# Gate decays of a linear-attention stage as products with constant 0/1 matrices, without scans

## The chip, the core and the metric

The kernel runs on one core of one Trainium2 chip. The metric is the device time of one execution in microseconds (us): the kernel before takes 1326.52 us, the median of three runs from 1323.62 to 1327.46.

Engine names in this text: PE is the matrix engine and PEld its weight loads, DVE the vector engine, ACT the scalar engine with the exponentials, POOL the third elementwise engine, SP the queue that issues DMAs.

## The reference

One layer of a diffusion backbone over 1024 latent tokens and 256 context tokens of width 1024. A mixer has two head groups side by side, gated linear attention (GLA, 4 heads, keys of 64, values of 128) and a state-space group (SSD); behind them come an output projection and a SwiGLU part. Shifts, scales and gates of both halves come from a modulation vector (`w_mod`). The change is in the GLA group, which runs forward and backward over the tokens:

```python
g_f = log_sigmoid(lr_f @ gla_wg_f + gla_bg_f) / 16.0        # g_b likewise; lr has 16 columns a direction

def step(s, inp):                                           # one chunk of _gla_scan
    qc, kc, vc, gc = inp
    cum = jnp.cumsum(gc, axis=1)
    inter = einsum("blhk,bhkv->blhv", qc * exp(cum), s)
    diff = cum[:, :, None] - cum[:, None, :]
    decay = exp(where(mask, diff, -inf))                    # lower triangle
    att = einsum("bihk,bjhk,bijhk->bhij", qc, kc, decay)
    intra = einsum("bhij,bjhv->bihv", att, vc)
    tot = cum[:, -1]
    s_new = s * exp(tot)[..., None] + einsum("blhk,blhv->bhkv", kc * exp(tot[:, None] - cum), vc)
    return s_new, inter + intra
```

So five things need exponentials of sums of gate steps `g`: queries against the state (`cum`), keys into the state (`tot - cum`), the whole chunk (`tot`), and for pairs of tokens inside a chunk the difference of two `cum`, split between query and key.

## The kernel before, in words

The program is one list of steps for all engines. Tile pools and a scheduler put each engine's instructions in an order; each engine then works its own list from the top. The GLA part works in two passes over pairs of heads, `gla_pair(p)` for p = 0 and 1, with 128 channels of a pair on the partitions and the 1280 tokens (`TT`) in ten chunks of 128.

`gates(p)` (L1080) makes, per direction `d`, the running sums of the gate steps, channel-major: three matmuls of `W96` with `LRT` (L1093), two DVE passes, Exp and Ln on ACT over all 1280 columns, one more DVE pass, and a scan along the tokens that a mask of ones and zeros (`rmask`) starts anew in each chunk. It leaves `cum[0]` and `cum[1]`.

Everything else takes differences of `cum`. `khat(d)` makes the keys into the state: DVE subtracts, ACT takes the exponential, POOL multiplies with `kT`, and ten transposes on PE turn the result token-major in `states(d)`, where 20 matmuls and DVE steps (L1165) run the state through the chunks.

Inside a chunk, pairs of tokens are split by levels, `LEVELS = (64, 32, 16, 8, 4, 2, 1, 0)`: at level 64 one half of a chunk meets the other half, at 32 quarters meet, and at the last a token meets itself. `operands(li)` makes one level's scaled queries `eq` and keys `ek` of 1024 columns: two subtractions on DVE (for `eq`) and two on POOL (for `ek`), an exponential of each on ACT, the product of `eq` with the queries on DVE and that of `ek` with the keys on POOL:

```python
V.tensor_tensor(eq, eq, qp, MUL)                                         # L1200
(V if p == 0 and li == 0 else G).tensor_tensor(ek, ek, kp, MUL)          # L1201
```

`products(li)` (L1204) multiplies `eq` with `ek` on PE in 64 matmuls of 64 columns, f32, and `place` (L1218) puts the wanted part into `Ad` with predicated copies on DVE. After the last level `At` holds a chunk's whole table. Then `qe` (queries against the state), and `outputs(hh, i)` (L1268): four groups of twelve f32 matmuls of `At`, `qe`, `St` and `v`, an RMS norm and the gate `r`.

Other work is put between these steps. `F` is a list of projections (units v, k, q, r, z; `proj` with three f16 matmuls of a split product, L198 to L200, called k1, q1 and so on for pair 1), from which `F.fill(us)` takes some steps and `F.need(name)` the rest of one unit. Fillers write to two PSUM banks of their own (`pf`); all else turns through six banks with `psum()`. In pair 1 the output projection `wo` (`out_mm`) and side work (`side(n)`) take the fillers' place. Side work loads and splits `w_out` and makes the modulation vectors: `mod_steps(piece)` (L1001) loads eight row blocks of `w_mod` of 512 KB into a `wst` buffer (L1005) and adds each to `macc` on DVE (L1008, L1010); `mod_row(2)` (L1013) and `mod_col(4)` (L1030) finish them with matmuls against ones, the latter at L1034. Its eight blocks are piece 4. Behind the GLA part `out_tile(t)` finishes 128 tokens of the mixer: it loads `x` (L1353) and stores `x2d` (L1375).

Ahead of the GLA part stands the SSD part, whose pool gives the buffers for masks. Weights that are split into two f16 are made by DVE at L193.

## Time and profile before

| | us | share of the span |
|---|---|---|
| median of three runs | 1326.52 | |
| profiled execution, its own time | 1326.59 | |
| span of its records | 1324.9 | |
| PE busy | 1179.8 | 89% |
| PE weight loads busy | 656.6 | 50% |
| DVE busy | 944.8 | 71% |
| ACT busy | 596.0 | 45% |
| POOL busy | 332.9 | 25% |
| DMA | 139.81 MB, mean 106 GB/s | |

PE is the busy engine over the whole program. A busy share is a mean over stretches of different kinds, so what follows below is cut at the steps of the GLA part: gates of pair 0 from 346.7 us, first product of a level at 380.8, levels of pair 0 to 421.3, its outputs to 472.3, levels of pair 1 to 529.6, its outputs to 578.5, and then the first tiles of `out_tile` to 606.6. The granted clock of PE is given as a share of 2.4 GHz; 0.50 is the other of its two levels, 1.2 GHz, and a stretch between the two holds some of each.

### The profile page before, as it was taken

To read this page: it belongs to the slowest core of one execution; us is meant where nothing else is said; L and a number is where in the kernel's file an instruction comes from. 1 tells how busy PE (TensorE), PEld (TensorE's weight loads), DVE (VectorE), ACT (ScalarE), POOL (GpSimd) and SP (SyncE) were. 2 spreads that over 40 slices of the span, in tenths; PEclk is the share of its full clock that TensorE was granted. 3 is DMA by queue.
4 is the path that set the end of the run, shared out by engine and by line. 5 is a ranking of instruction groups with operands and counts; after the bars stand their busy time and mean duration, and the time that the engine had idled before them with its cause. 6 is when DMAs were issued, how large, how long until landed. Compare 5 with 4: busy or idle time off the path is not lost. (4 is left out here: it accounts for less than half of the span.)

```text
span 1324.9 us, 19466 instructions
## 1 busy us (share of the span) xinstructions
PE 1179.8 (89%) x7640; PEld 656.6 (50%) x7640; DVE 944.8 (71%) x1487; ACT 596.0 (45%) x1104; POOL 332.9 (25%) x245
## 2 busy tenths in 40 slices
PE   5996899999948977977895799999999999999997
PEld 3563565767726666544442344444444444444444
DVE  8688887577699877666679975677775656855347
ACT  5346535445454555342654343444443334443432
POOL 1234051231086273110227311122121111300011
PEclk9997799999968898697997999999999999999999
DMA  9600310101200002447622542355542225320416
GB/s 316 201 18 16 80 45 21 49 1 61 71 33 2 1 1 84 155 157 265 202 76 94 176 143 80 112 175 172 178 143 72 72 80 198 135 100 13 148 67 207
DMA packets 90201, 139.81 MB, mean 106 GB/s; under 512 B 7560, under 2 KB 61053, under 8 KB 90109
## 3 DMA queue, kind: packets, MB, share of 16 engines
q1 hardware_dynamic: 90109, 138.56, 31.9%
q8 instruction: 60, 0.98, 0.3%
q14 instruction: 32, 0.26, 0.1%
HBM read 117.05 MB, written 20.97 MB: 104 GB/s over the span
## 5 line engine op out<-in xcount | busy, mean ns | idle before, releaser
L198 PE MATMUL ps<-T,wS 128*128 128x512 f16 x264 | 102.1, 387 | 14.3 <-DVE u L1566 7.9
L199 PE MATMUL ps<-T,wS 128*128 128x512 f16 x264 | 101.7, 385 | 4.0 <-DVE T L1395 4.0
L200 PE MATMUL ps<-T,wS 128*128 128x512 f16 x264 | 101.6, 385 | 0.0
L1676 DVE TENSOR_TENSOR ah<-hid,ah 128x512 f16<-128x512 f32 x66 | 50.6, 769 | 54.4 <-ACT ah L1675 54.4
L1455 DVE SCALAR_TENSOR_TENSOR wS<-S,wS 128x512 f16<-128x512 f32 x88 | 66.5, 768 | 29.3 <-ACT wS L1454 29.2
L1454 ACT ACTIVATE wS<-S 128x512 f16<-128x512 f32 x88 | 54.3, 628 | 56.1 <-PE ps L200 29.2
L1675 ACT CAST ah<-hid 128x512 f16<-128x512 f32 x66 | 40.4, 617 | 85.3 <-PE ps L200 46.5
L1455 DVE SCALAR_TENSOR_TENSOR wA<-wst,wA 128x512 f16<-128x512 f32 x66 | 54.9, 835 | 29.3 <-ACT wA L1454 29.2
L1454 ACT ACTIVATE wA<-wst 128x512 f16<-128x512 f32 x66 | 41.4, 628 | 59.0 <-PE ps L200 36.3
L1471 POOL TENSOR_TENSOR S<-wst,S 128x512 f32<-128x512 f32 x22 | 32.6, 1483 | 140.2 <-DVE S L1470 88.1
L199 PEld LDWEIGHTS <-wS 128*128 128x128 f16 x352 | 34.9, 99 | 58.0 <-issue 19.1
L198 PEld LDWEIGHTS <-wS 128*128 128x128 f16 x352 | 35.0, 99 | 51.6 <-DVE u L1566 8.4
L1469 POOL TENSOR_TENSOR S<-wst 128x512 f32<-128x512 f32 x22 | 31.0, 1409 | 115.0 <-DVE wS L1455 95.4
L200 PEld LDWEIGHTS <-wS 128*128 128x128 f16 x352 | 35.0, 99 | 47.5 <-issue 7.4
L483 DVE SCALAR_TENSOR_TENSOR acc<-xin,cwcol,acc 128x945 f32<-128x945 f32 (+2 forms) x40 | 50.2, 1273 | 0.4
L1214 PE MATMUL ps<-eq,ek 64*64 64x64 f32 x896 | 22.0, 245 | 29.9 <-DVE ek L1201 14.5
L199 PEld LDWEIGHTS <-hl 128*128 128x128 f16 x448 | 42.8, 98 | 9.9 <-issue 5.5
L198 PEld LDWEIGHTS <-hl 128*128 128x128 f16 x448 | 42.8, 98 | 8.8 <-issue 3.1
L200 PEld LDWEIGHTS <-hl 128*128 128x128 f16 x448 | 42.8, 98 | 5.0 <-issue 0.4
L199 PE MATMUL ps<-wo,oT 128*128 128x512 f16 x112 | 44.4, 397 | 0.0
L198 PE MATMUL ps<-wo,oT 128*128 128x512 f16 x112 | 44.4, 397 | 0.0
L1762 POOL TENSOR_TENSOR ot<-C,macc 128x512 f32<-128x512 f32 x8 | 10.7, 1340 | 133.5 <-PE ps L200 117.9
(538 smaller groups left out, 3667.4 us busy)
## 6 DMA issues: line engine op xcount, KB each, us to landing
wmst<-in_w_mod_dram SPq DMA_DIRECT2D x32, 512.0 KB, 4.2
wst<-in_w_gate_dram SPq DMA_DIRECT2D x26, 512.0 KB, 3.6
wst<-in_w_up_dram SPq DMA_DIRECT2D x26, 512.0 KB, 3.6
wdb<-in_w_down_dram SPq DMA_DIRECT2D x22, 512.0 KB, 5.1
x<-in_x_dram SPq DMA_DIRECT2D x16, 512.0 KB, 6.6
wm<-in_w_mod_dram SPq DMA_DIRECT2D x8, 1024.0 KB, 10.5
t32d<-wdt SPq DMA_DIRECT2D x11, 512.0 KB, 3.4
t14d<-wdt SPq DMA_DIRECT2D x11, 512.0 KB, 4.8
```

Of the source, the lines that this page charges most:

```text
L198: PE.matmul(ps, lh, rh, start=start, stop=False, skip_group_check=on)
L199: PE.matmul(ps, lh, rl, start=False, stop=False, skip_group_check=on)
L200: PE.matmul(ps, ll, rh, start=False, stop=stop, skip_group_check=on)
L483: V.scalar_tensor_tensor(acr[:, r0:r1, q0:q1], xr[:, r0 + dr:r1 + dr, q0 + dc:q1 + dc], cw, acr[:, r0:r1, q0:q1], MUL, ADD)
L1214: PE.matmul(out_[hh][64 * b:64 * b + 64, ci, :], ek[hs, j0:j0 + 64], eq[hs, i0:i0 + 64], start=True, stop=True)
L1454: S.activation(w[:, 0], src, AF.Copy, scale=SW)
L1455: V.scalar_tensor_tensor(w[:, 1], src, SW, w[:, 0], MUL, SUB)
L1469: G.tensor_tensor(s3, b["A11"], b["A21"], SUB)
L1471: G.tensor_tensor(s4, b["A12"], s2, SUB)
L1675: S.copy(dst[:, 0], src)
L1676: V.tensor_tensor(dst[:, 1], src, dst[:, 0], SUB)
L1762: eng.tensor_tensor(ot[:, c0:c0 + n], c, m5r[0][:, m:m + n], MUL)
```

## The change

The gate steps stay token-major and are never summed. For two chunks at a time `gates(p)` multiplies `LRT` (now the stationary side) with `W96` for both directions, adds the bias (loaded as `bt`, broadcast to all partitions), takes the log-sigmoid as min(x, 0) - ln(1 + exp(-|x|)) and scales it by `SG` = 16; `gh` holds it as two f16 parts, the rounded value and the rest.

Every exponent is then a matmul of `gh` with a constant matrix of zeros and ones in f16, one matmul for each part, summed in PSUM (`decay_of`). The running sum of a chunk is `gh` times a triangle (`inc`), what is left to its end is `gh` times the strict triangle (`exc`), the whole chunk is `gh` times a column of ones (`ones16`), and the sums that level `li` needs are `gh` times one of the masks `lvm[:, li]`, which `level_masks()` makes once, in the SSD part, with 28 products on POOL and seven comparisons on DVE. ACT reads the sums from PSUM and takes the exponential with the scale `EG` = 1/256.

So the scans, the subtractions on DVE and POOL and `rmask` go. `khat` works token-major now: the keys `kT` are transposed (ten transposes a pair, not twenty), and DVE multiplies them with the exponentials in PSUM. The products of `ek` are all on DVE. A level of `eq` and `ek` takes four PSUM banks of 512 columns; at level 1 the keys need no factor and `ek` is `kp` itself. In the loop over the levels the sums of level li + 2 are made behind the products of level li, and its factors are applied behind `place`; `khat`, `totals` and `states` stand at other levels than before.

The diff, with short parts left out:

```diff
@@ -36 +36 @@
 SHID = 4.0
 INV = 1.0 / (SW * SH)
 SL = 2048.0
+SG = 16.0
+EG = 1.0 / (16 * SG)
...
@@ -84 +86 @@
...
+    ones16 = cons.tile([P, 1], F16, name="ones16")
+    G.tensor_copy(ones16, ones[:, 0:1])
 
...
@@ -122 +126 @@
...
-    rmask = mc.tile([P, TT], F16, name="rmask")
-    V.memset(rmask, 1.0)
-    V.memset(rmask.rearrange("p (n l) -> p n l", l=P)[:, :, 0:1], 0.0)
+    lvm = mc.tile([P, 7, 2, 2, 64], F16, name="lvm")
+    t16 = mc.tile([P, 4, P], F16, name="t16")
+    inc, exc = (t16[:, 0], t16[:, 1]), (t16[:, 2], t16[:, 3])
+    def level_masks():
...
+        for i, nm in enumerate(("le", "ge", "gt", "lt")):
+            G.tensor_copy(t16[:, i], tri[nm])
+        for li in range(7):
+            lv = 64 >> li
+            bl = ssd.tile([P, P], F16, tag="xw", bufs=3, name="bl")
+            V.tensor_scalar(bl, xi, float(lv), None, ALU.is_lt)
+            b4 = bl.rearrange("p (n a l) -> p n a l", a=2, l=lv)
+            for i, (d, x, a) in enumerate(((0, 0, 1), (1, 0, 0), (0, 1, 0), (1, 1, 1))):
+                G.tensor_tensor(lvm[:, li, d, x].rearrange("p (n l) -> p n l", l=lv),
+                                t16[:, i].rearrange("p (n a l) -> p n a l", a=2, l=lv)[:, :, a], b4[:, :, a], MUL)
...
@@ -725 +748 @@
...
+    level_masks()
...
@@ -1064 +1088 @@
...
-    cums = {}
+    bt = gla.tile([P, 2, 2, P], F32, name="bt")
+    for d, bg in enumerate((gla_bg_f, gla_bg_b)):
+        nc.sync.dma_start(bt[:, :, d], bg.to_broadcast((P, 256)).rearrange("p (q c) -> p q c", q=2))
+    gs = {}
 
     def gates(p):
 
-        cum = cums[p] = []
...
+        gh = gs[p] = gla.tile([P, 2, NCH, 2, P], F16, tag="gh", bufs=1, name=f"gh{p}")
+        for t0 in (2, 4, 6, 8, 0):
+            ps = psum().rearrange("p (t d c) -> p t d c", t=2, d=2)
+            for j in range(2):
+                PE.matmul(ps[:, j], LRT[:, (t0 + j) * P:(t0 + j + 1) * P], W96[:, :, p * P:(p + 1) * P],
+                          start=True, stop=True)
+            x_ = gla.tile([P, 2, 2, P], F32, tag="gx", bufs=2, name="gx")
+            l_ = gla.tile([P, 2, 2, P], F32, tag="gl", bufs=2, name="gl")
+            V.scalar_tensor_tensor(x_.rearrange("p t d c -> p t (d c)"), ps.rearrange("p t d c -> p t (d c)"), INV,
+                                   bt[:, p].rearrange("p d c -> p (d c)")[:, None, :].to_broadcast((P, 2, 256)), MUL, ADD)
+            S.activation(l_, x_, AF.Abs)
+            S.activation(l_, l_, AF.Exp, scale=-1.0)
+            S.activation(l_, l_, AF.Ln, bias=1.0)
+            V.scalar_tensor_tensor(x_, x_, 0.0, l_, ALU.min, SUB)
+            V.tensor_scalar(x_, x_, -4000.0, SG, ALU.max, MUL)
+            S.copy(gh[:, 0, t0:t0 + 2], x_)
+            V.tensor_tensor(gh[:, 1, t0:t0 + 2], x_, gh[:, 0, t0:t0 + 2], SUB)
+            if t0 in (4, 8):
+                F.fill(FILLS[9])
 
     def gla_pair(p, after_levels):
         v = gla.tile([P, NCH, 256], F32, tag="v", bufs=1, name=f"v{p}")
@@ -1115 +1137 @@
         evac_v[0] = False
         if p == 0:
             gates(0)
-        cum = cums[p]
+        gh = gs[p]
         F.need(f"k{p}")
         F.need(f"q{p}")
-        kts, ets, St = [], [], []
...
+        St = []
+        khts = [gla.tile([P, NCH, P], F32, tag="kh", bufs=2, name=f"kht{d}") for d in range(2)]
+        ets = sm.tile([P, 2, NCH], F32, tag="et", name="et")
+        def decay_of(out_, t, d, mask):
+            for s in range(2):
+                PE.matmul(out_, gh[:, s, t, d], mask, start=(s == 0), stop=(s == 1))
+        def khat(n):
+            t0, t1 = ((2, 6), (6, 10), (0, 2))[n]
+            w = (t1 - t0) * P
+            pk = psum()
+            for t in range(t0, t1):
+                PE.transpose(pk[:, (t - t0) * P:(t - t0 + 1) * P], kT[p][:, t * P:(t + 1) * P], ident)
+            for d in range(2):
+                pa = psum()
+                for t in range(t0, t1):
+                    for s in range(2):
+                        PE.matmul(pa[:, (t - t0) * P:(t - t0 + 1) * P], exc[d], gh[:, s, t, d],
+                                  start=(s == 0), stop=(s == 1))
+                kh = khts[d][:, t0:t1].rearrange("p t c -> p (t c)")
+                S.activation(kh, pa[:, :w], AF.Exp, scale=EG)
+                V.tensor_tensor(kh, kh, pk[:, :w], MUL)
+        def totals():
+            pt_ = psum()[:, :2 * NCH].rearrange("p (d n) -> p d n", d=2)
+            for d in range(2):
+                for t in range(NCH):
+                    decay_of(pt_[:, d, t:t + 1], t, d, ones16)
+            S.activation(ets, pt_, AF.Exp, scale=EG)
 
         def states(d):
-            kh, et = kts[d], ets[d]
...
+            kht, et = khts[d], ets[:, d]
             F.fill(FILLS[10])
             F.need(f"v{p}")
             st = gla.tile([P, NL, P], F32, tag=f"St{d}", bufs=1, name=f"St{d}")
@@ -1172 +1207 @@
         Ad = [gla.tile([P, NL, 64], F32, tag="Ad", bufs=2, name=f"Ad{hh}") for hh in range(2)]
         ops = {}
 
+        def decays_of_level(li):
+            lv = LEVELS[li]
+            if li % 2 and lv:
+                eq = ar.tile([P, T], F32, tag="oG", bufs=4, name="eq")
+                ek = ar.tile([P, T], F32, tag="oG", bufs=4, name="ek") if lv > 1 else kp
+            else:
+                eq = gla.tile([P, T], F32, tag="eq", bufs=2, name="eq")
+                ek = gla.tile([P, T], F32, tag="eq", bufs=2, name="ek") if lv > 1 else kp
+            ops[li] = eq, ek
+            if lv == 0:
+                S.activation(eq, qp, AF.Copy, scale=2.0)
+                return
+            for b in range(2):
+                ps = [psum() for _ in range(1 + (lv > 1))]
+                for c in range(4):
+                    t = NC_CTX + 4 * b + c
+                    for d in range(2):
+                        for x_, px in enumerate(ps):
+                            decay_of(px[:, c * P:(c + 1) * P].rearrange("p (n a l) -> p n a l", a=2, l=lv)[:, :, x_ ^ 1 ^ d],
+                                     t, d, lvm[:, li, d, x_].rearrange("p (n l) -> p n l", l=lv))
+                for px, e in zip(ps, (eq, ek)):
+                    S.activation(e[:, b * 512:b * 512 + 512], px, AF.Exp, scale=EG)
         def operands(li):
             lv = LEVELS[li]
-            if li % 2:
...
+            eq, ek = ops[li]
+            if lv:
+                V.tensor_tensor(eq, eq, qp, MUL)
+            if lv > 1:
+                V.tensor_tensor(ek, ek, kp, MUL)
 
         def products(li):
 
@@ -1231 +1269 @@
                         o = slice(64 * b, 64 * b + 64)
                         (S.copy if b else G.tensor_copy)(At[hh][o, :, o], Ad[hh][o])
 
+        decays_of_level(0)
         operands(0)
-        khat(0)
+        decays_of_level(1)
+        operands(1)
         F.fill(FILLS[11])
-        operands(1)
-        extra = {0: lambda: khat(1), 2: lambda: states(0), 4: lambda: states(1)}
+        extra = {0: (lambda: khat(0), lambda: khat(1)), 1: (lambda: khat(2), totals), 2: (lambda: states(0),),
+                 4: (lambda: states(1),)}
         for li in range(len(LEVELS)):
             prods = products(li)
             if li + 2 < len(LEVELS):
+                decays_of_level(li + 2)
+            place(li, prods)
+            if li + 2 < len(LEVELS):
                 operands(li + 2)
-            place(li, prods)
             F.fill(FILLS[12])
-            if li in extra:
-                extra[li]()
+            for fn in extra.get(li, ()):
+                fn()
             if p == 1 and li == 3:
                 F.need("v1")
                 F.need("r1")
@@ -1253 +1295 @@
         qe = []
         for d in range(2):
             e = gla.tile([P, T], F32, tag="eq", bufs=2, name="qe")
-            S.activation(e, cum[d][:, TC:], AF.Exp, scale=1.0 / 16)
-            (V if d == 0 else G).tensor_tensor(e, e, qp, MUL)
+            for b in range(2):
+                ps = psum()
+                for c in range(4):
+                    decay_of(ps[:, c * P:(c + 1) * P], NC_CTX + 4 * b + c, d, inc[d])
+                S.activation(e[:, b * 512:b * 512 + 512], ps, AF.Exp, scale=EG)
+            V.tensor_tensor(e, e, qp, MUL)
             qe.append(e)
         if p:
             r_silu(p)
```

The change also moves work that it does not name. Three places follow.

On PE, in the levels of pair 0, rows of `L1214` are the products of a level, and `w_k` with `pf` is the projection of the keys of pair 1 (k1), a filler. Before:

```order
L199 LDWEIGHTS w_k_4569
L199 MATMUL pf<-hl_168,w_k_4569 128x512
L1214 MATMUL ps<-eq,ek 64x64 x64
L200 LDWEIGHTS w_k_4569
L200 MATMUL pf<-hl_168,w_k_4569 128x512
L198 LDWEIGHTS w_k_4569
L198 MATMUL pf<-hl_161,w_k_4569 128x512
```

After, the half of a level's products that stands there is followed by the sums of a later level (`lvm` with `gh`), not by fillers:

```order
L1252 MATMUL ps<-eq,ek 64x64 x32
L1150 LDWEIGHTS gh_3800
L1150 MATMUL ps<-lvm,gh_3800 128x4x16
L1150 LDWEIGHTS gh_3800
L1150 MATMUL ps<-lvm,gh_3800 128x4x16
```

And k1 stands later on PE, from the gates of pair 1 on (`W` with `LRT`), which the program makes with the outputs of pair 0; the names `w_k` and `hl` are as above:

```order
L1113 MATMUL ps<-W_3793,LRT 128x256
L1113 LDWEIGHTS LRT
L1113 MATMUL ps<-W_3793,LRT 128x256
L221 LDWEIGHTS w_k_5183
L221 MATMUL pf<-hl_162,w_k_5183 128x512
L222 LDWEIGHTS w_k_5183
L222 MATMUL pf<-hl_162,w_k_5183 128x512
```

So the projection of k1 has moved from between the products of pair 0 to behind its levels.

On SP, at the end of the GLA part, `nr` and `br` are the rows that `mod_row(2)` loads, `wmst` the row blocks of `w_mod`, `x` and `x2d` the loads and stores of `out_tile`. Before:

```order
L1019 DMA nr<-in_norm_mix_post_dram 128x1024
L1020 DMA br<-in_b_mod_dram 128x1024
L1353 DMA x_6023<-in_x_dram 128x1024
L1005 DMA wmst<-in_w_mod_dram 128x1024 x2
L1375 DMA x2d_5998<-x_6023 128x1024
L1005 DMA wmst<-in_w_mod_dram 128x1024 x2
L1353 DMA x_6074<-in_x_dram 128x1024
L1005 DMA wmst<-in_w_mod_dram 128x1024 x2
L1375 DMA x2d_5999<-x_6074 128x1024
```

After:

```order
L1043 DMA nr<-in_norm_mix_post_dram 128x1024
L1044 DMA br<-in_b_mod_dram 128x1024
L1029 DMA wmst<-in_w_mod_dram 128x1024 x8
L1399 DMA x_7186<-in_x_dram 128x1024
L1399 DMA x_7237<-in_x_dram 128x1024
L1399 DMA x_7287<-in_x_dram 128x1024
L1421 DMA x2d_7161<-x_7186 128x1024
L1029 DMA wmst<-in_w_mod_dram 128x1024 x3
L1421 DMA x2d_7162<-x_7237 128x1024
```

The eight blocks of piece 4 now go out in one row behind `br`, ahead of the first load of `x`, where they went out two at a time between loads and stores of tiles.

## Rows read from the trace of the kernel before

**Rows 1.** Stretches: window, length, busy us of each engine, granted clock, DMA share, GB/s.

```profile
346.70:366.40 19.70, 19.53 (x151) 14.70 (x151) 19.08 (x21) 9.35 (x13) 4.59 (x3) 1.00 0.00 1
366.40:380.80 14.40, 0.02 (x4) 0.02 (x4) 14.40 (x7) 6.58 (x8) 13.25 (x5) 0.59 0.00 0
380.80:421.30 40.50, 29.67 (x625) 24.10 (x626) 38.40 (x45) 18.39 (x24) 28.04 (x15) 0.77 0.08 28
421.30:472.30 51.00, 47.07 (x266) 32.52 (x266) 43.97 (x59) 27.40 (x68) 18.65 (x10) 0.90 0.00 1
472.30:529.60 57.30, 43.91 (x789) 36.13 (x788) 42.26 (x46) 29.77 (x42) 29.29 (x16) 0.91 0.15 49
529.60:578.50 48.90, 46.05 (x199) 28.06 (x198) 28.89 (x54) 18.76 (x60) 5.59 (x3) 0.79 0.32 107
578.50:606.60 28.10, 13.84 (x66) 7.97 (x64) 19.14 (x38) 8.23 (x20) 4.65 (x3) 0.78 0.81 280
```

**Rows 2.** Waits of PE, 340 to 607 us: us in total, times, longest us.

```profile
PE ps L1214 <- DVE ek L1201: 14.5, 1, 14.5
PE ps L1034 <- DVE macc L1010: 14.3, 1, 14.3
```

**Rows 3.** Timeline of PE, SSD part: start us, us, instruction.

```profile
228.10 0.20 PE L198 MATMUL ps<-xsl,Eh 128*128 128x64 f16 x1
...
228.43 0.19 PE L200 MATMUL ps<-xsl,Eh 128*128 128x64 f16 x1
```

**Rows 4.** Timeline of PE, two matmuls of 512 columns.

```profile
224.78 0.38 PE L198 MATMUL pf<-hl,w_q 128*128 128x512 f16 x1
224.99 0.38 PE L199 MATMUL pf<-hl,w_q 128*128 128x512 f16 x1
```

**Rows 5.** Lines by form, 200 to 330 us: busy us, mean ns; idle.

```profile
L199 PEld LDWEIGHTS <-Eh 128*128 128x128 f16 x64 | 5.8, 98 | 0.0
```

**Rows 6.** Lines by form, 340 to 545 us: busy us, mean ns; idle, releaser.

```profile
L1201 POOL TENSOR_TENSOR ek<-ek,kT 128x1024 f32<-128x1024 f32 x13 | 34.0, 2614 | 19.1 <-ACT ek L1199 19.1
...
L1228 DVE COPY_PREDICATED Ad<-lm,ps 128x512 f32<-128x512 uint8 x24 | 16.8, 724 | 0.9 <-PE ps L1214 0.9
...
L1165 DVE SCALAR_TENSOR_TENSOR St<-St,et,ps 128x128 f32<-128x128 f32 x28 | 9.4, 337 | 0.4
...
L193 DVE SCALAR_TENSOR_TENSOR w_v<-st_v,w_v 128x1024 f16<-128x1024 f32 x2 | 3.2, 1634 | 0.0
...
L1283 DVE TENSOR_TENSOR r<-r,ps 128x512 f32<-128x512 f32 x4 | 2.7, 678 | 0.0
...
L1226 ACT COPY Ad<-ps 128x512 f32<-128x512 f32 x4 | 2.1, 590 | 0.0
```

**Rows 7.** Timeline of DVE, products of pair 0.

```profile
373.55 3.36 DVE L1200 TENSOR_TENSOR eq<-eq,qT 128x1024 f32<-128x1024 f32 x1
...
380.65 1.21 DVE L1200 TENSOR_TENSOR eq<-eq,qT 128x1024 f32<-128x1024 f32 x1
```

**Rows 8.** Stretches of output matmuls in pair 0 and pair 1.

```profile
427.10:435.50 8.40, 8.40 (x50) 6.46 (x50) 6.92 (x11) 5.89 (x11) 0.00 (x0) 1.00 0.01 3
542.00:558.00 16.00, 16.00 (x59) 10.99 (x59) 6.98 (x16) 6.04 (x30) 0.00 (x0) 0.50 0.45 153
```

**Rows 9.** Timeline of SP, end of the GLA part.

```profile
559.81 0.33 SPq L1020 DMA_DIRECT2D br<-in_b_mod_dram  x1
578.68 0.33 SPq L1353 DMA_DIRECT2D x<-in_x_dram  x1
```

**Rows 10.** DMA issues of the page: KB each, us to landing.

```profile
wmst<-in_w_mod_dram SPq DMA_DIRECT2D x32, 512.0 KB, 4.2
```

**Rows 11.** Timeline of PE behind the GLA part, with the idle time before.

```profile
603.15 3.54 PE L1034 MATMUL ps<-ones,macc 128*128 128x1 f32 x16 [14.26 <-DVE macc L1010]
```

**Rows 12.** Timeline of POOL, taps of the SSD part.

```profile
110.48 8.95 POOL L497 TENSOR_TENSOR acc<-acc,tm 128x1008 f32<-128x1008 f32 x4 [7.10 <-ACT tm L495]
```

**Rows 13.** Timeline of PE, products of one level.

```profile
472.34 1.16 PE L1214 MATMUL ps<-eq,ek 64*64 64x64 f32 x64
```

More of the change, by code (lines that the diff above doesn't have):

```diff
@@ L1066, in dit_layer_kernel @@
     gla = es_gla.enter_context(tc.tile_pool(name="gla", bufs=1))
-    wg32 = gla.tile([96, 2, 256], F32, tag="mu", bufs=2, name="wg32")
+    wg32 = gla.tile([96, 2, 256], F32, tag="gl", bufs=2, name="wg32")
     V.memset(wg32, 0.0)
@@ L1076, in dit_layer_kernel @@
     LEVELS = (64, 32, 16, 8, 4, 2, 1, 0)
-    cums = {}
+    bt = gla.tile([P, 2, 2, P], F32, name="bt")
+    for d, bg in enumerate((gla_bg_f, gla_bg_b)):
+        nc.sync.dma_start(bt[:, :, d], bg.to_broadcast((P, 256)).rearrange("p (q c) -> p q c", q=2))
+    gs = {}
     def gates(p):
-        cum = cums[p] = []
-        for d in range(2):
-            gt = gla.tile([P, TT], F32, tag="kh", bufs=2, name="gt")
-            bcol = vc("bgf" if d == 0 else "bgb", p)
-            b4 = sm.tile([P, 1], F32, tag="b4", name="b4")
-            V.tensor_scalar(b4, bcol, 1.0 / INV, None, MUL)
-            nb = sm.tile([P, 1], F32, name="nb")
-            V.tensor_scalar(nb, bcol, -1.0, None, MUL)
-            cm = gla.tile([P, TT], F32, tag=f"cum{d}", bufs=1, name=f"cum{d}")
-            for o0, n in (LAT0, LAT1, CTX):
-                ps = psum()
-                PE.matmul(ps[:, :n], W96[:, d, p * P:(p + 1) * P], LRT[:, o0:o0 + n], start=True, stop=True)
-                m = cm[:, o0:o0 + n]
-                V.tensor_scalar(m, ps[:, :n], b4, 0.0, ADD, ALU.min)
-                V.scalar_tensor_tensor(gt[:, o0:o0 + n], m, -2.0, ps[:, :n], MUL, ADD)
-            S.activation(gt, gt, AF.Exp, scale=-INV, bias=nb)
-            S.activation(gt, gt, AF.Ln, bias=1.0)
-            V.scalar_tensor_tensor(gt, cm, INV, gt, MUL, SUB)
-            if d == 0:
-                V.tensor_tensor_scan(cm, rmask, gt, 0.0, MUL, ADD)
-            else:
-                V.tensor_tensor_scan(cm[:, ::-1], rmask, gt[:, ::-1], 0.0, MUL, ADD)
-            cum.append(cm)
-            F.fill(FILLS[9])
@@ L1117, in gla_pair @@
             gates(0)
-        cum = cums[p]
+        gh = gs[p]
         F.need(f"k{p}")
         F.need(f"q{p}")
-        kts, ets, St = [], [], []
-        def khat(d):
-            c3 = ch3(cum[d])
-            tot = c3[:, :, P - 1:P] if d == 0 else c3[:, :, 0:1]
-            kh = gla.tile([P, TT], F32, tag="kh", bufs=2, name="kh")
-            V.tensor_tensor(ch3(kh), tot.to_broadcast((P, NCH, P)), c3, SUB)
-            S.activation(kh, kh, AF.Exp, scale=1.0 / 16)
-            G.tensor_tensor(kh, kh, kT[p], MUL)
-            et = sm.tile([P, NCH], F32, tag=f"et{d}", name="et")
-            S.activation(et, tot.rearrange("p n o -> p (n o)"), AF.Exp, scale=1.0 / 16)
-            kts.append(kh)
-            ets.append(et)
@@ L1135, in states @@
-        def states(d):
-            kh, et = kts[d], ets[d]
-            kht = gla.tile([P, NCH, P], F32, tag="kht", bufs=1, name="kht")
-            for t0, t1 in ((0, 4), (4, 8), (8, 10)):
-                ps = psum()
-                for t in range(t0, t1):
-                    PE.transpose(ps[:, (t - t0) * P:(t - t0 + 1) * P], kh[:, t * P:(t + 1) * P], ident)
-                S.copy(kht[:, t0:t1, :], ps[:, :(t1 - t0) * P].rearrange("p (t c) -> p t c", c=P))
+        St = []
+        khts = [gla.tile([P, NCH, P], F32, tag="kh", bufs=2, name=f"kht{d}") for d in range(2)]
@@ L1175, in operands @@
         def operands(li):
             lv = LEVELS[li]
-            if li % 2:
-                eq = ar.tile([P, T], F32, tag="oG", bufs=4, name="eq")
-                ek = ar.tile([P, T], F32, tag="oG", bufs=4, name="ek") if lv else None
-            else:
-                eq = gla.tile([P, T], F32, tag="eq", bufs=2, name="eq")
-                ek = gla.tile([P, T], F32, tag="eq", bufs=2, name="ek")
-            if lv == 0:
-                S.activation(eq, qp, AF.Copy, scale=2.0)
-                ops[li] = eq, kp
-                return
```

21 lines of the change are left out of this document (5 added, 16 removed).

## The prediction

> **What bounds the kernel now.** I read the busy table cut into stretches first. The change works in the two passes of the GLA part, from 346.7 to 578.5 us, and there PE is busy 186 us of 232: gates of pair 0 (346.7 to 366.4), a hole with PE idle (to 380.8), levels of pair 0 (to 421.3), outputs of pair 0 with filler projections (to 472.3), levels of pair 1 (to 529.6), outputs of pair 1 (to 578.5). In the levels of pair 0 it is DVE that is full, 38.40 us of 40.50; in the outputs of pair 0 it is PE, 47.07 of 51.00; in the levels of pair 1 none is full, but POOL has 29.29 and stands in the chain of every level [rows 1]. The seventh row, 578.5 to 606.6, is behind the GLA part: PE works 13.84 us of 28.10 there. Then I read what PE waits for. Two waits stand far above the rest: 14.5 us for the first `ek` product, which is the hole, and 14.3 us in front of `mod_col` (L1034) for `macc` (L1010) [rows 2]. So the profile says three things. DVE and POOL hold up the levels, PE is nearly full between them, and a wait on weights that has nothing to do with gates lies behind.
>
> **What is added, on PE.** Per pair there are 416 matmuls of 64 columns for the level decays (six levels of 64, one of 32), 40 of 128 columns in `khat`, 32 of 128 columns for `qe`, 40 of one column for the totals: 528, each with its own 128x128 f16 weight load. The trace has this shape in the SSD part: twelve run from 228.10 to 228.43, 0.030 us apart [rows 3]. A 128-column one has no row; it lies between that 0.030 and the 0.215 from one 512-column matmul to the next [rows 4], and by columns it is near 0.06, which I take. That makes 12.5 + 4.3 + 1.2 = 18 us a pair, 36 us in all. The ten transposes fewer per pair I leave out. A weight load by itself takes 0.098 us [rows 5], three times the 0.030, so loads run beside matmuls and beside each other. The Trainium skill ("TensorE: Matmul & The Clock Gate", section LDWEIGHTS) gives the load of P columns as P/1.2 ns, which is 107 ns here and 113 us for 1056 pairs; the spacing in the trace disagrees, and the measurement decides.
>
> **What it costs and gives, stretch by stretch.**
>
> Gates and hole, 34.1 us before. A chunk of two token tiles passes eight steps in line, four on DVE and four on ACT, each 512 columns, with 0.68 us on DVE and 0.59 on ACT as the nearest rows [rows 6]: about 5 us. Two chunks are in flight (two buffers), and each engine gives a chunk 2.4 to 2.7 us, so two rounds take about 15.5 us for the four chunks that level 0 needs, to 362.5. Then come 1 us of decays, 2.4 us of four exponentials in ACT's queue and two DVE products of 1.21 us, the time that the same product takes when POOL does not work beside it (3.36 beside it) [rows 7]. First product at 368.5 instead of 380.8: -12. Bounds: DVE alone the limit, -17; no overlap of chunks at all, +4.
>
> Levels of pair 0. DVE afterwards: 11 products at 1.21 (13.3), six `khat` products (four of 0.68, two of about 0.4: 3.5), twelve predicated copies at 0.72 (8.7), 16 state steps at 0.34 and two copies (6.0), two weight splits at 1.63 (3.3) [rows 6, 7]: 34.8 us against 38.4. PE has 29.67 us and gets 14. `khat`, the decays and the products now share the six PSUM banks, and I give 5 us for that: 0, bounds -4 and +16 (next part).
>
> Outputs of pair 0. The order shows that 44 of the k1 matmuls stood in the hole and between the levels, and now all stand here: 44 x 0.215 = 9.5 us [rows 4]. The 128 decay matmuls of the first two levels of pair 1 add 3.8. PE had 3.9 us free here: +9 (+5 to +13). ACT gets 20 gate passes and eight exponentials of 0.59, 16.5 us on 27.4, which PE's 60 us cover.
>
> Levels of pair 1. PE gets 8.6 + 4.3 + 1.2 us and gives nine `wo` matmuls (1.9 us) to the next stretch; +12.2 against 13.4 us free. POOL's part, 2.61 us of `ek` product per level [rows 6] and the two subtractions, is gone. With PE full instead: 0 (-5 to +11).
>
> Outputs of pair 1. The nine `wo` matmuls: +1.9. From 542 to 558 the granted clock is 0.50, the 1.2 GHz level, though PE is busy all the time; it fell after a stretch with PE mostly idle and rose after f16 matmuls had come again. The same f32 output matmuls ran at 1.00 in pair 0 [rows 8]. In the new order `wo` matmuls stand after two output groups, not after three, so one group of 4.2 us (half of 8.40) may be spared its second 4.2; I take 3 of it. Together -1 (-8 to +4).
>
> Behind GLA: the wait of 14.3. The eight `wmst` loads of piece 4 feed `macc`, and PE's queue stands still at `mod_col` until the eighth is added. Before, SP's queue has the load of `x` ahead of them; it went out at 578.68, 18.9 us after `br` at 559.81 [rows 9], and the order of before has loads and stores of tiles between them. In the new order all eight stand right behind `br`. They need a `wst` buffer each (three of them), a landing of 4.2 us [rows 10] and a DVE step: eight loads in three buffers are three rounds of 5.5 to 6, say 18 us from 561, with a few us for DVE's own queue: 583 to 587. PE reaches `mod_col` at 588.9 (603.15 less the wait of 14.26) [rows 11]. What is late next is DVE with tile 0 and 1, whose `x` comes a little later; PE does not wait for it as long as the six banks last. -12 (-14 to 0).
>
> Ahead of 346.7: 28 mask products of 64 columns on POOL, which does 1008 columns in 2.24 us, so 0.14 by columns and perhaps 0.4 with a fixed part: 4 to 11 us, against 7.1 us that POOL waits there [rows 12]. The seven comparisons on DVE are small. And `wg` no longer queues behind the 512 KB load of `r`. -1 (-3 to +5).
>
> Sum: -12 + 0 + 9 + 0 - 1 - 12 - 1 = -17 us, on the profiled run's 1326.59 (span 1324.9 and 1.7 around it): 1309.6. The median of 1326.52 is the same within 0.1.
>
> **Rivals.**
> 1. The loads move but the wait stays: DVE adds `macc` in its own order, and the second half of the eight waits behind tile 0. For it: the steps stand between steps of tile 0 in DVE's order. Against: those are short. -17 + 12 = -5: 1321.5.
> 2. Slower: the bank turn. A level takes two banks for products and four for decays, which is all six. If PE can't run ahead, a level is the sum of 1.16 us of products [rows 13], 1.9 of decays, 2.4 of exponentials and 3.9 on DVE, 9.3 us, where the levels take 5.1 (40.5/8) and 7.2 (57.3/8) now. With two thirds of that excess in pair 0 and half in pair 1 it is +22 + 8 = 30 us, 1340; it decides from 1.1 us a level on, where the 17 us are used up. Against it: the exponentials of a level free their banks while DVE still multiplies an earlier one.
> 3. The clock stays at 1.00: PE has no hole of 14 us any more and more f16 work. The 16 us at 0.50 in the outputs of pair 1 are then 8, and a few us come back in both level stretches: -13 more, 1296.5. Against it: the 0.50 there came after PE waited for `At`, and that wait is still in the order.
> 4. The weight loads do not overlap in this place: 1056 x 0.098 = 103 us in place of 36: 1377. The twelve pairs 0.030 apart speak against it [rows 3, 5]. [...]
>
> **How the numbers follow.** Forecast 0.50, rival 1 0.17, rival 2 0.14, rival 3 0.17, rival 4 0.02. A measurement of this kernel can tell about 0.3%, 4 us, from no change: 1322.5 to 1330.5. Faster: the forecast nearly whole (0.49), rival 3 (0.17), half of rival 1 (0.09): 0.75. Same: the rest of rival 1 (0.08), some of rival 2 (0.04): 0.12. Slower: 0.13. The forecast's own range is 1300 to 1319; from rival 3 to the middle of rival 2, with 2 in 10 left out, it is 1290 to 1331.
>
> **What would show it.** Right: first `ek` product within 24 us of the first gate matmul; the level decays 0.03 us apart; the outputs of pair 0 longer by about 9 us with PE full; no wait over 4 us of `mod_col` on `macc`; POOL nearly empty in the levels. Wrong: decay matmuls 0.06 or 0.1 apart, PE waiting for exponentials or `khat` products in each level (rival 2), or the 14 us at `mod_col` still there (rival 1).

## The result, and the profile after

The changed kernel takes 1286.2 us, the median of four runs (1285.16 to 1287.1); the kernel before took 1325.07 beside it. The ratio is 0.9706 (95% interval 0.9685 to 0.9727): 39 us faster, where 17 us were forecast and 1290 was the lower end of the range. The profiled execution took 1286.45 us, its span is 1284.7.

The stretches of the changed kernel, cut at the same steps as [rows 1] (gates and what stood in the hole are one row here, and the last row ends with `mod_col`, which before ended at 606.6); columns: window, length, PE, PEld, DVE, ACT and POOL busy with counts, granted clock, DMA share, GB/s:

```profile
348.40:369.30 20.90, 17.87 (x245) 14.65 (x245) 13.13 (x21) 16.06 (x32) 0.00 (x0) 1.00 0.23 77
369.30:403.80 34.50, 31.89 (x987) 29.06 (x988) 29.92 (x49) 19.65 (x37) 0.00 (x0) 1.00 0.12 34
403.80:460.90 57.10, 56.62 (x476) 39.78 (x474) 30.91 (x58) 33.27 (x86) 1.16 (x2) 1.00 0.00 1
460.90:513.60 52.70, 48.69 (x1135) 44.68 (x1134) 30.81 (x44) 27.28 (x48) 0.00 (x0) 0.97 0.20 61
513.60:557.70 44.10, 42.62 (x242) 26.33 (x243) 32.49 (x57) 20.49 (x63) 2.15 (x2) 1.00 0.54 178
557.70:570.10 12.40, 12.31 (x65) 6.41 (x64) 10.93 (x23) 4.12 (x11) 1.55 (x1) 1.00 0.83 279
```

PE is busy for 86 to 99% of every row, POOL is nearly empty, and the clock, which was 0.77, 0.90, 0.91, 0.79 and 0.78 in the rows of before, is 1.00 in all but one. To see how much of the gain each of these is, I cut the time of each stretch into three: PE idle; the price of half clock (in windows of one us, PE's busy time times one minus the granted clock, since `wo` matmuls stand 0.43 us apart in rows at 0.50 and 0.215 apart in rows at 1.00); and the rest, PE's work at full clock.

| stretch | length before, after | idle | price of half clock | work at full clock |
|---|---|---|---|---|
| gates and hole | 34.1, 20.9 | 14.6, 3.0 | 0.0, 0.0 | 19.5, 17.9 |
| levels, pair 0 | 40.5, 34.5 | 10.8, 2.6 | 8.5, 0.0 | 21.1, 31.9 |
| outputs, pair 0 | 51.0, 57.1 | 3.9, 0.5 | 5.1, 0.0 | 42.0, 56.6 |
| levels, pair 1 | 57.3, 52.7 | 13.4, 4.0 | 5.1, 1.7 | 38.8, 47.0 |
| outputs, pair 1 | 48.9, 44.1 | 2.8, 1.5 | 10.2, 0.0 | 35.8, 42.6 |
| to `mod_col` | 28.1, 12.4 | 14.3, 0.1 | 1.7, 0.0 | 12.1, 12.3 |
| sum | 259.9, 221.7 | 59.8, 11.7 | 30.6, 1.7 | 169.3, 208.3 |

So 39 us of work came in (36 were forecast), and 48 us of idle time and 29 us of half clock went: 39 - 48 - 29 = -38. With 1.7 us lost ahead of the gates and 3.7 gained behind `mod_col` that is the 40.2 us between the spans. My forecast had 36 of the first number, 49 of the second (what its -16 for these stretches leaves) and 3 of the 29.

The sum puts the half clock about a tenth too high. The 199 matmuls of the outputs of pair 1 kept PE busy for 46.05 us in the kernel before [rows 1] and for 36.98 in a run that had the same 199 at 1.00 (b_at, below): 9.1 us less, where the sum gives 10.2. So the 29 are nearer 26, and the 39 of work nearer 36.

What PE waits for, 340 to 607 us (total, times, longest), beside [rows 2]:

```profile
PE ps L1150 <- ACT eq L1232: 2.8, 1, 2.8
PE ps L1058 <- DVE macc L1034: 2.7, 1, 2.7
PE ps L1150 <- ACT gh L1124: 2.3, 2, 2.1
```

The two waits of 14.5 and 14.3 us are gone; the longest is 2.8, of a decay matmul for a bank that ACT still reads, and it has the one dip of the clock behind it (0.97 in the fourth row above). The way from the first gate matmul to the first product, on PE's timeline:

```profile
348.48 1.25 PE L1113 MATMUL ps<-W,LRT 96*128 96x256 f16 x10 [0.63 <-issue]
...
361.29 2.49 PE L1150 MATMUL ps<-lvm,gh 128*128 128x64 f16 x64 [0.25 <-ACT gh L1124]
...
364.96 0.99 PE L1150 MATMUL ps<-lvm,gh 128*128 128x64 f16 x28
...
369.34 1.16 PE L1252 MATMUL ps<-eq,ek 64*64 64x64 f32 x64 [0.44 <-DVE ek L1240]
```

20.9 us, where 34.0 stood before. 64 decay matmuls with 64 weight loads take 2.49 us, some 0.036 apart; in the faster row it is 0.03 (28 in 0.99 us, with about 0.2 for the last one's end). And the loads of `w_mod`, on SP's timeline, beside [rows 9]:

```profile
535.09 0.33 SPq L1044 DMA_DIRECT2D br<-in_b_mod_dram  x1
545.03 14.17 SPq L1029 DMA_DIRECT2D wmst<-in_w_mod_dram  x8
559.30 1.32 SPq L1399 DMA_DIRECT2D x<-in_x_dram  x3
```

The first load of piece 4 goes out 12.7 us ahead of the end of the GLA part (557.7). In the kernel before it went out 0.6 us behind that end (578.5):

```profile
579.11 0.84 SPq L1005 DMA_DIRECT2D wmst<-in_w_mod_dram  x2
```

### The profile page after: what moved, and what is told of

Same layout as the page of the kernel before. It is cut to its first block, busy times and chain, and to the rows that moved or that the text cites. A ratio compares the mean times of both kernels' runs of the same rounds, so it can differ in the third digit from the quotient of the medians.

```text
span 1284.7 us, 21607 instructions
## 1 busy us (share of the span) xinstructions
PE 1189.7 (93%) x8684; PEld 673.5 (52%) x8684; DVE 897.4 (70%) x1486; ACT 602.4 (47%) x1158; POOL 249.5 (19%) x233
## 5 line engine op out<-in xcount | busy, mean ns | idle before, releaser
L1721 ACT CAST ah<-hid 128x512 f16<-128x512 f32 x66 | 40.5, 618 | 85.3 <-PE ps L223 46.5
L506 DVE SCALAR_TENSOR_TENSOR acc<-xin,cwcol,acc 128x945 f32<-128x945 f32 (+2 forms) x40 | 48.9, 1240 | 0.4
L222 PEld LDWEIGHTS <-wA 128*128 128x128 f16 x264 | 25.9, 98 | 35.6 <-issue 5.2
L221 PE MATMUL ps<-wo,oT 128*128 128x512 f16 x112 | 44.2, 395 | 0.0
L222 PE MATMUL ps<-wo,oT 128*128 128x512 f16 x112 | 44.0, 393 | 0.0
L223 PE MATMUL ps<-wo,oT 128*128 128x512 f16 x112 | 43.8, 391 | 0.0
## 6 DMA issues: line engine op xcount, KB each, us to landing
wm<-in_w_mod_dram SPq DMA_DIRECT2D x8, 1024.0 KB, 10.4
```

The costliest lines, as they stand in the source:

```text
L221: PE.matmul(ps, lh, rh, start=start, stop=False, skip_group_check=on)
L222: PE.matmul(ps, lh, rl, start=False, stop=False, skip_group_check=on)
L223: PE.matmul(ps, ll, rh, start=False, stop=stop, skip_group_check=on)
L506: V.scalar_tensor_tensor(acr[:, r0:r1, q0:q1], xr[:, r0 + dr:r1 + dr, q0 + dc:q1 + dc], cw, acr[:, r0:r1, q0:q1], MUL, ADD)
L1721: S.copy(dst[:, 0], src)
```

## The experiments

Twelve kernels ran. Theory A says that PE's pauses bring the clock down, so that a pause costs itself and work at half clock behind it; theory B, that the clock has other reasons. The rest is on the price of each part.

**a_pause.** The changed kernel with a pause in front of one output group, which is issued behind the matmul of `z` (the diffs here leave out short parts, marked `...`):

```diff
+            if p == 1 and hh == 0 and i == 0:
+                z = sm.tile([P, P], F32, tag="jkg", bufs=1, name="zz")
+                nc.sync.dma_start(z, qe[1][:, 896:1024])
+                zi = tc.keep_in_program_order(PE.matmul(psum_f("wm")[:, :P], z, z, start=True, stop=True))
...
+                es_z.enter_context(tc.issue_after(zi.ins))
```

> The changed kernel with one pause added: ahead of the first output matmul of pair 1, PE waits for one small matmul whose operand is copied by a DMA from the second qe product (64 KB, not used otherwise). Theory A (a pause of PE costs itself and a stretch at half clock behind it): a pause of 2 to 4 us, the outputs of pair 1 at 0.50 for 8 to 20 us, 1292 to 1299 against 1286. Theory B (a pause costs only itself): 1287 to 1290, with the clock at 1.00.

1299.86 us, 13.7 more than the changed kernel (ratio to before 0.9812, 0.9783 to 0.9841). The wait, and the stretch behind it:

```profile
PE wm L1321 <- DMA zz<-qe: 5.0, 1, 5.0
```

```profile
514.00:524.00 10.00, 4.60 (x121) 4.00 (x118) 9.93 (x16) 7.35 (x10) 3.16 (x2) 0.78 0.44 127
524.00:536.00 12.00, 12.00 (x43) 7.42 (x43) 7.98 (x10) 2.82 (x11) 0.00 (x0) 0.61 0.75 255
536.00:569.00 33.00, 33.00 (x173) 19.86 (x172) 15.47 (x34) 10.15 (x42) 0.00 (x0) 1.00 0.32 109
```

PE is busy without a gap from 524 to 536, and the clock is 0.61. The pause was longer than expected, 5.0 us; the half clock behind it cost 5.0 more (the same sum as in the table). Theory A holds here: the price of a pause was twice its length. The other 3.7 us the runs do not sort out; several waits just ahead are longer too (3.8 us for `eq`, 2.8 in the changed kernel).

**a_hi.** Half of the added matmuls left out: the sums use the rounded part of `gh` alone, so the exponents are less exact.

```diff
-            for s in range(2):
-                PE.matmul(out_, gh[:, s, t, d], mask, start=(s == 0), stop=(s == 1))
+            PE.matmul(out_, gh[:, 0, t, d], mask, start=True, stop=True)
...
```

> The changed kernel with half of the added matmuls left out: the sums are made of the rounded f16 part of gh alone (528 matmuls and weight loads fewer of 1056; the low part is computed but not used, so the exponents are less exact). Theory (PE is full in the GLA part now, so added matmuls cost what they take, 30 us for all): 1270 to 1277 against 1286, the outputs of pair 0 and the levels shorter by 5 and 9 us. Rival (DVE and ACT hold the levels, and PE's time there is free): 1282 to 1288, with more idle time of PE and perhaps half clock.

1280.30 us (0.9668, 0.9644 to 0.9692): 6 less than the changed kernel, between the two theories. The stretches tell why. The levels of both pairs and the outputs of pair 0 are shorter (30.40, 46.90 and 53.30 us against 34.5, 52.7 and 57.1), 13.7 us together, 13.0 of it PE's work at full clock, so the work was fully paid. But then:

```profile
507.30 0.49 PE L1319 MATMUL ps<-v,At 128*128 128x128 f32 x2 [1.47 <-POOL At L1268]
```

```profile
508.00:534.00 26.00, 26.00 (x82) 16.94 (x82) 11.46 (x22) 5.95 (x30) 0.00 (x0) 0.50 0.40 140
```

With PE earlier, POOL's last copy into `At` was late by 1.47 us, and the 26 us behind it ran at half clock, at a price of 13.7 us in that stretch by the same sum. In this trace the copy took 3.21 us, and the one before it 0.61 (the next expectation has 0.84 for each). The clock was back at 1.00 from 536 on, in a run of 18 f16 matmuls of `wo`.

**a_hi_at.** a_hi, and the last copies into `At` of pair 1 on DVE:

```diff
-                        (S.copy if b else G.tensor_copy)(At[hh][o, :, o], Ad[hh][o])
+                        (S.copy if b else (V if p else G).tensor_copy)(At[hh][o, :, o], Ad[hh][o])
```

> a_hi (sums of the rounded part alone) with one more edit: in pair 1 the two last copies into At, which POOL makes in 0.84 us each, are made by DVE. In a_hi PE waited 1.47 us for the second of them, and the next 27 us, the outputs of pair 1, ran at a granted clock of 0.50, at a price of 13.7 us. Theory A (the clock falls because of pauses of PE just ahead): the pause is under 0.6 us, the outputs of pair 1 run at 1.00 and the time is 1265 to 1271 against 1280. Theory B (with less f16 work in the levels the clock falls there in any case): 1278 to 1282.

1273.50 us (0.9621, 0.9594 to 0.9648), 6.8 less than a_hi, and 2.5 above the range of theory A. The pause is 0.3 us, and the same window of the trace reads:

```profile
508.00:534.00 26.00, 24.20 (x129) 15.64 (x129) 16.79 (x35) 8.59 (x41) 0.00 (x0) 1.00 0.54 181
```

129 matmuls in the time of 82; the order of the work on PE is nearly the same. The 221 matmuls from the sums for `qe` to the end of the outputs of pair 1 keep PE busy for 40.65 us, and in a_hi for 52.69, so the half clock cost 12.0 us there. Theory A holds for the clock, with 6.8 us of them at the end: new waits of 1.8 and 1.4 us for `macc` follow, the second with 3.4 us of half clock behind it. The first has none, though f32 matmuls follow it too:

```profile
524.74 0.70 PE L1048 MATMUL ps<-macc,ones 128*128 128x512 f32 x1 [1.80 <-DVE macc L1034]
```

```profile
528.00:534.00 6.00, 6.00 (x33) 3.74 (x33) 3.34 (x9) 1.98 (x10) 0.00 (x0) 1.00 0.55 169
```

This is the fastest kernel of this study, with the exponents less exact.

**b_at.** The same edit of `At` in the kernel before.

> The kernel before with the same one edit (the two last copies into At on DVE in pair 1). There PE waited 1.8 us for POOL's copy ahead of the outputs of pair 1, and 10.2 us of half-clock price followed. Theory A: 1311 to 1318 against 1325, the outputs of pair 1 at 1.00 for the most part. Theory B (pauses of 2 to 3 us in the levels just ahead suffice to bring the clock down): 1322 to 1326.

1318.22 us (0.9957, 0.9939 to 0.9975), 6 us faster by one line, at the upper end of theory A's range, and the outputs of pair 1 take 41.70 us at full clock instead of 48.9:

```profile
528.60:570.30 41.70, 36.98 (x199) 22.19 (x199) 29.52 (x56) 18.71 (x60) 2.35 (x1) 1.00 0.38 125
```

But the pause did not go away. On PE's timeline, first of the kernel before, then of b_at:

```profile
536.23 0.46 PE L1275 MATMUL ps<-v,At 128*128 128x128 f32 x2 [1.83 <-POOL At L1232]
537.72 0.71 PE L1275 MATMUL ps<-v,At 128*128 128x128 f32 x4 [1.02 <-POOL At L1232]
```

```profile
535.75 1.02 PE L1275 MATMUL ps<-v,At 128*128 128x128 f32 x6 [2.32 <-DVE At L1232]
536.60 0.38 PE L198 MATMUL ps<-wo,oT 128*128 128x512 f16 x1
```

One pause of 2.32 us left the clock up; 1.83 and 1.02 with a few matmuls between them brought it down. The edit also moved work: three f16 matmuls of `wo` stand behind the first `At` products of b_at (the first is shown), where the kernel before has f32 matmuls from 536.2 to 555.4. Whether the single pause or these three kept the clock up is not shown. Pauses matter, but how long or how close they must be, and what has to stand behind them, is not settled by these runs.

**a_at.** The control: the edit of `At` in the changed kernel.

> Control: the changed kernel with the same edit. PE waits only 0.37 us there and the clock is 1.00 in the outputs of pair 1, so by every theory nothing changes: 1284 to 1288. If it is faster by more than 3 us, the copies were worth something by themselves, and a_hi_at and b_at must be read with that.

1285.17 us (0.9712, 0.9688 to 0.9736), as expected: the copies are worth nothing where nobody waits for them.

**b_warm.** Idle work for the clock's sake, in the kernel before:

```diff
+    def warm(n):
+        ps = psum_f("wm").rearrange("p (a c) -> p a c", a=4)
+        for i in range(n):
+            ins = PE.matmul(ps, ident16, ident16[:, None, :].to_broadcast((P, 4, P)), start=True, stop=True)
...
```

> The kernel before with idle-time matmuls added: 180 f16 matmuls of 512 columns on a constant, whose results nobody reads, pinned on PE where it waits (60 at the first level of pair 0, 20 and 6 at two later levels, 8 and 12 in pair 1, 14 ahead of the outputs of pair 1, 60 at mod_col). Nothing else is changed. Theory A (the granted clock falls because PE pauses, and 33 us of the PE time from 346.7 to 631.4 us are its price): the clock is 1.00 in most of this stretch, and the time falls by 12 to 25 us though work is added, 1300 to 1313. Theory B (the clock falls for another reason, the f32 matmuls say, or for no reason in the order of the work): the clock is as before and the time 1325 to 1335.

1324.10 us (1.001, 0.999 to 1.0029): no difference, in neither theory's range. From the gates to the second `mod_col` (284.7 us before, 289.2 here) the price of half clock fell from 33 to 22 us and idle time from 60 to 35, but 40 us of work came in, 39 of it the 180 added matmuls at 0.215. They did not lie only in the pauses: the first 60 ran ahead of filler projections, which then waited for ACT, and the hole stayed in part:

```profile
PE ps L1228 <- DVE ek L1210: 8.5, 1, 8.5
PE pf L205 <- ACT v L295: 8.2, 2, 5.5
```

Theory A has the sign of the clock right and the time wrong. This run does not tell the theories apart by itself.

**b_p4first.** The kernel before, with piece 4 listed first: `+    side(8, side_work2)` ahead of the loop over output tiles.

> The kernel before with one edit: the eight loads of piece 4 and their additions are listed ahead of the first output tile, so SP has them in one row behind br; gates, scans and levels are those of before. Theory (the wait of 14.3 us at mod_col is a matter of load order alone, and PE behind it is then not at half clock): the wait is under 4 us and the time 1310 to 1314 against 1325. Rival (DVE adds late all the same, or the tiles' own x loads become late): 1321 to 1327.

1338.74 us (1.0114, 1.0087 to 1.014): slower, against both. The edit also moved `mod_col` ahead of 48 `wo` matmuls on PE, and the loads did not start earlier (576.9), since SP waited there for the end of the outputs of pair 1:

```profile
SPq L1005 <- DVE r L1285: 11.1, 1, 11.1
...
SPq L1005 <- PE ps L604: 7.0, 1, 7.0
```

```profile
PE ps L1034 <- DVE macc L1010: 29.0, 2, 18.8
```

**b_p4gla.** The clean form of the same question: the loads stand in the side work of the GLA part, `mod_col` keeps its place.

```diff
-    side_work2 = mod_steps(4, m4a) + [lambda: mod_col(4, m4a)] + mod_steps(3, m3a) + [lambda: mod_col(3, m3a)]
+    side_work += mod_steps(4, m4a)
+    side_work2 = [lambda: None] * 8 + [lambda: mod_col(4, m4a)] + mod_steps(3, m3a) + [lambda: mod_col(3, m3a)]
...
-                side(3)
+                side(5)
```

> The kernel before with the eight loads of piece 4 moved into the side work of the GLA part (behind mod_row(2), in the buffers of that part), while mod_col stays at its place on PE, behind the 48 wo matmuls. In b_p4first two things stood in the way: mod_col had moved ahead of those 48 matmuls, and the first load waited for the last transposes of the GLA part. Theory (what counts is when the first of these loads goes out): it goes out at 565 or before instead of 579, the wait at mod_col is under 4 us, 1307 to 1314 against 1324. Rival (loads that run beside the outputs of pair 1 cost there what they give, or another wait takes over): 1319 to 1328.

1313.98 us (0.9925, 0.9900 to 0.9951), 11 less, at the upper end of the theory's range. The loads go out from 556.1 on, and the 14.3 us at `mod_col` are gone; a wait of 7.6 for the earlier `macc` of `mod_row` takes part of it back:

```profile
PE ps L1024 <- DVE macc L1010: 7.6, 1, 7.6
...
PE ps L1034 <- DVE macc L1010: 1.5, 1, 1.5
```

**a_p4late.** The reverse, in the changed kernel: the loads of piece 4 and of `x` and the stores of `x2d` are pinned in the order of before.

```diff
+            if piece == 4:
+                tc.keep_in_program_order(dm)
...
+        if t < 2:
+            tc.keep_in_program_order(dx)
+            side(2, side_work2)
...
+        if t == 1:
+            side(1, side_work2)
```

> The changed kernel with one edit: the loads of piece 4 go out two at a time between the loads of x and the stores of x2d, as in the kernel before. Theory (the order of these loads is worth the wait at mod_col and some half clock behind it): the wait is back with 10 to 15 us, 1297 to 1303 against 1286. Rival (with the GLA part denser the loads are early enough in any order): 1285 to 1290.

1307.16 us (0.9876, 0.9853 to 0.9900), 21 more than the changed kernel, above what the theory gave:

```profile
PE ps L1060 <- DVE macc L1036: 25.0, 1, 25.0
```

But this is not the clean reverse. The edit also took `mod_col` ahead of the 48 `wo` matmuls that stand before it in both kernels, as in b_p4first. On PE's timeline, first of the changed kernel, then of a_p4late:

```profile
567.68 0.38 PE L223 MATMUL ps<-wo,oT 128*128 128x512 f16 x1
568.14 1.92 PE L1058 MATMUL ps<-ones,macc 128*128 128x1 f32 x16
```

```profile
555.76 1.04 PE L627 MATMUL ps<-ident,r 128*128 128x128 f32 x8
581.77 3.58 PE L1060 MATMUL ps<-ones,macc 128*128 128x1 f32 x16 [24.98 <-DVE macc L1036]
585.21 0.59 PE L221 MATMUL ps<-wo,oT 128*128 128x512 f16 x1
```

In the changed kernel these 48 take 10.4 us, from 557.5 to 567.9. With them ahead the wait would have been some 14.6 us and the loss some 11; both are estimates from these rows. With the 11 of b_p4gla that puts the place of eight loads, which the diff does not name, at over a quarter of the 39 us.

**b_sum.** Gates alone: the gates of the changed kernel, and `cum` by one product with the triangle and a copy on ACT; everything behind is that of before.

```diff
+        for t0, t1 in ((2, 6), (6, 10), (0, 2)):
+            w = (t1 - t0) * P
+            for d in range(2):
...
+                for t in range(t0, t1):
+                    for s in range(2):
+                        PE.matmul(ps[:, (t - t0) * P:(t - t0 + 1) * P], gh[s][:, t, d], inc[d],
+                                  start=(s == 0), stop=(s == 1))
+                S.activation(cum[d][:, t0 * P:t1 * P], ps[:, :w], AF.Copy, scale=1.0 / SG)
```

> One part of the change alone: the gates of the changed kernel (token-major, split in two f16), and the running sums by one product with the triangle per direction, copied to SBUF by ACT; no scans. Levels, khat, qe and the products on POOL are those of before, and so is the load order of piece 4. Theory (the hole is a matter of gates in chunks; the pauses in the levels, and the half clock behind them, belong to the subtractions and POOL's products and stay): first product of a level 20 to 26 us behind the first gate matmul instead of 34, the wait of 14.3 still there, 1308 to 1318 against 1324. Rival 1 (with the hole closed the clock stays up in all of the GLA part): 1290 to 1302. Rival 2 (the hole only moves): 1320 to 1330.

1332.02 us (1.0054, 1.0033 to 1.0075): 7 us slower than before, and 2 above the range of rival 2. The first product came at 31.2 us instead of 34.0, and the hole moved on to the third level:

```profile
PE ps L1231 <- DVE eq L1217: 17.6, 5, 12.1
PE ps L1039 <- DVE macc L1015: 14.6, 1, 14.6
```

Rival 2 of that expectation holds: gates in chunks close nothing by themselves. In the 12.1 us DVE works without a gap: four subtractions of the third level (1.52 us each), a weight split (3.91) and the products. The changed kernel has no such subtractions and makes its sums on PE two levels ahead; that this is what closes the hole there is argued, as `khat` and the order changed with it.

**a_ekpool.** The products of `ek` back on POOL: `+ (V if p == 0 and li == 0 else G).tensor_tensor(ek, ek, kp, MUL)`.

> The changed kernel with the products of ek back on POOL (but for the first level of pair 0, as in the kernel before). Theory (2.6 us of POOL in every level's chain and a slower DVE beside it bring pauses of PE and half clock back): 1296 to 1315 against 1286, levels of both pairs longer. Rival (DVE is relieved of 14 us and POOL has nothing else to do, so the levels are as before or shorter): 1278 to 1289.

1290.13 us (0.9735, 0.9718 to 0.9753): 4 us more, between the theory and the rival. The levels of pair 0 are 2.5 us longer, those of pair 1 as before the edit, at full clock but for 0.97:

```profile
369.60:406.60 37.00, 32.00 (x987) 29.06 (x988) 28.23 (x44) 19.59 (x37) 13.24 (x5) 1.00 0.10 32
463.80:516.30 52.50, 48.45 (x1134) 44.51 (x1134) 28.40 (x41) 27.44 (x48) 12.98 (x5) 0.97 0.22 73
```

So in the changed kernel POOL's product alone does not hold the levels, and most of the gain there does not come from it. What it costs in the kernel before is not tested.

**a_at_p4gla.** a_at with the loads placed as in b_p4gla.

> The changed kernel with the copies into At on DVE and the loads of piece 4 in the side work of the GLA part, as in b_p4gla, so that the loads of piece 3 come earlier too. Theory: the wait of 2.7 us at the second mod_col and the half clock behind it (1 us) go, 1280 to 1284. Rival (the additions on DVE and the loads come beside the outputs of pair 1 and make a new pause there, with half clock behind it): 1286 to 1300.

1293.92 us (0.9768, 0.9739 to 0.9798): the rival. PE waited 4.4 us for the first `macc`, with a dip to 0.57 behind it, and 6.8 later for `hf` on DVE. Here the place that the scheduler had found for these loads was better than mine.

## Why the prediction was wrong

The sign and most of the parts were right, the size was not: -39 for -17, with the time 4 us below the range. The step that failed is the term for the half clock: the sum took 3 us back, in one stretch, and some 26 to 29 came back, in five. By its steps:

- **Gates and hole, -12.** -13.2, and 20.9 us to the first product for the 22 of the working. The reason was half of it: b_sum shows that chunks alone move the hole.
- **Levels of pair 0 and 1, 0 and 0.** -6.0 and -4.6. The work that came in was 10.8 and 8.2 us net. That fits, within about 1 us, the 14 us of new matmuls of each pair less what went: 21 k1 matmuls (24 shorter ones of `w_v` came) and ten transposes in pair 0, twelve `wo` matmuls (the working has nine) and ten transposes in pair 1. Idle time fell by 8.2 and 9.4. The 0 of each was this sum without the clock: 8.5 and 5.1 us of half clock were in these rows, as 0.77 and 0.91 in [rows 1], and I gave none of it back. How much of it the closed pauses gave back and how much the added f16 matmuls is not parted; a_hi, with half of these, has 1.00 in both. In pair 0 the working also had the wrong limit, DVE with 34.8 us and 5 for the banks; DVE was busy 29.92 us of the 34.50, and PE 31.89.
- **Outputs of pair 0, +9.** +6.1. 14.6 us of work came in for 13.3 (9.5 and 3.8), into 3.4 us of idle time and 5.1 of half clock, of which I counted only the first.
- **Outputs of pair 1, -1.** -4.8. Here the failed step shows most plainly: "I take 3 of it" of the half clock that [rows 8] show. All of it went, 10.2 us by the sum and 9.1 by b_at. The step let the clock follow from which matmuls stand there (f16 or f32); what brings it down there is a wait for `At` just ahead, as a_hi and a_hi_at show in the changed kernel; in the kernel before, b_at points the same way, with what it leaves open. The prediction's reason against rival 3, that the wait for `At` is still in the order, was read from an order, which does not say whether anyone is late: in the changed kernel PE stands idle there for 0.37 us.
- **Behind GLA, -12.** -15.7 in place of it, and the wait of 14.3 at 0 (a later one is 2.7). The mechanism (eight loads in three buffers, in time if they start behind `br`) held: they start at 545.0, the last is added at 568.0. The price of the loads alone is some 11 us by b_p4gla, and by the estimate from a_p4late. That x's load held SP back in the old order is shown; it waited itself for the last transposes of the GLA part:

```profile
SPq L1353 <- PE ps L604: 18.4, 1, 18.4
```

- **Ahead of 346.7, -1.** +1.7, within its bounds. Behind `mod_col`, where nothing was forecast, 3.7 us were gained: PE's idle time there is 6.2 us less and the half clock 3.0 more. No run isolates them.
- **Added matmuls.** 36 us forecast; a_hi took half of them away and 16.5 us of PE's work with them up to the end of the GLA part, so about 33. The pairs of 128 columns, put at 0.06 without a row, run 0.056 apart (24 in 1.50 us, less 0.2 for the end). Weight loads lie beside matmuls, and rival 4 is out. The 107 ns that the prediction takes from the Trainium skill ("TensorE: Matmul & The Clock Gate", section "LDWEIGHTS (loading the stationary operand)") is the time of one load and near the 0.098 us of [rows 5]; it says nothing on how far apart pairs stand, so the 0.030 does not speak against it.

```profile
515.51 1.50 PE L1150 MATMUL ps<-t,gh 128*128 128x128 f16 x24
```

Rival 3 (the clock stays at 1.00) is what happened, and it had 0.17. It was priced at 13 more than the forecast; the rows held 31 by the sum above. Its place was not beside the forecast but inside it: closing the pauses and keeping the clock went together here, as in a_pause and a_hi_at, and a sum that takes the first with full weight and the second with a sixth is not one case. Rival 2 (the bank turn) shows as one wait of 2.8 us, not 1.1 a level.

The Trainium skill ("TensorE: Matmul & The Clock Gate", section "A second HAM failure mode: psum-queue depth-cycling") says of another kernel that PE's small idle times between groups of matmuls come often enough to make the clock swing, and that the cost is paid between the bursts. a_hi and a_hi_at agree that a small idle time matters, with 12.0 us behind a wait of 1.47, but there the cost lies in the work itself, with PE busy; b_at, where 2.32 us cost nothing behind it, does not agree.

## What to carry to other kernels

Before summing a change that closes PE's pauses, work out the price of half clock in each stretch (busy time times one minus the granted clock): here 31 us by that sum, a tenth less by two pairs of runs, stood in rows that I had shown and not summed. A pause that opens just ahead of a long run of f32 matmuls can cost many times its length (1.47 us and 12.0 in a_hi; none for 1.80 in a_hi_at), so look at who is late there once everything else is faster. And compare the DMA queue's order too: eight loads that nobody meant to move carried over a quarter of this gain, and putting them by hand elsewhere lost part of it. When a run is to undo one thing, look in its trace for what else it moved: a_p4late and b_at each moved `wo` matmuls as well.
